# Outputs of an S5 scan: one 128-row product for two of 64 rows

## The chip, the cores and the metric

The kernel runs on one core of a Trainium2 chip. The metric is the device time of one execution in microseconds (us), the median of three runs. Engines: PE (TensorE, matrix products), DVE (VectorE), ACT (ScalarE), POOL (GpSimd), SP (SyncE, which here issues the transfers).

## What is computed

Two layers of a decoder, each with three head groups: HGRN2, gated linear attention and S5. 1,024 prompt tokens go through both layers, and 8 further sequences take one token each from a given state. The change concerns the third group, S5: 16 channel groups of 16 channels, each with 64 complex states x.

```
bu_re = einsum('gpc,btgc->btgp', bb_re, u);  bu_im likewise
x_t   = a * x_(t-1) + bu_t                    (complex, associative scan over t)
y     = einsum('gcp,btgp->btgc', C_re, x_re) - einsum('gcp,btgp->btgc', C_im, x_im) + D * u
```

The outputs y are a sum over 64 real and 64 imaginary parts per channel group.

## The kernel before

Tokens stand in the free dimension, 1,032 in blocks of 384, 384 and 264. Every projection is a loop (`gemm_tile`, L302) over tiles of 128 output channels: for each block, eight slices of the input, each with three products of fp32r halves (`hh`, `lo` by `wh`, `wl`) into a PSUM bank `ps_g`. The halves of the weights are made on the way by `do_split` (L274): ACT copies `wh`, and POOL and DVE in turn subtract to give `wl` (L289). DVE moves a finished bank out (L741).

The recurrences are Python generators ("threads"), and `tick()` lets each emit its next piece between the products of a tile. Slots of the on-chip memory are handed out by `alloc`, `release` and `need`. The order in the engines' queues is then set by the scheduler of the tile framework from the program's order and its own timeline.

`s5_thread` (L467) runs the third group, in two runs (`hf`) per layer of eight channel groups each. Two channel groups share the 128 partitions: `gp` 0 in rows 0 to 63, `gp` 1 in rows 64 to 127, four such pairs q. Tokens are cut into 128 pieces of 8, and a piece's state x is scanned over the pieces. One run goes like this:

- `E_` (powers of the state's rotation, POOL, L488 to L494), `PB` and `Bm` (input matrices), `Tm` (the kernel within a piece).
- `Vt` = `Bm` times the inputs `U` on PE (L558), evicted by ACT (L560).
- The rotation by `E_` on DVE and POOL gives `W_` (L574 to L580, tile name `s5W`); DVE scans it (L584), eight scans.
- The rotation back (`cmul`, six DVE operations, L591) writes the states `Xp` over `Vt` (tile name `s5V`), real parts in `Xp[:, 0]`, imaginary ones in `Xp[:, 1]`; the 8 further sequences' states are copied to columns 128 to 136 (L589).
- The output matrices `O_` (`s5O`, L604 to L609) are made by POOL and DVE.
- The outputs (L613 to L628): for each half q2 of the pairs, a bank `py[gp]` for each channel group sums products of 64 rows, two for each of two pairs (`ri` 0 and 1), and then the products by `Tm` (128 rows, L625). They are plain fp32, and each shows as two records of PE in the trace.

```
for ri in range(2):
    for gp in range(2):
        rr = slice(64 * gp, 64 * gp + 64)
        mm(o(gp, qq), O_[rr, ri, 2 * q2 + qq, :], Xp[rr, ri, 2 * q2 + qq, :], start=(qq + ri == 0), stop=False)
```

In this kernel, layer 0's first run has its outputs at 118 to 128 us and its second at 201 to 207 us; layer 1's are at 624 to 634 and 704 to 711 us.

Of the kernel before, what the change touches and what calls it, by code (L numbers as in the profile page):

```python
# [12 lines left out]
ALU = mybir.AluOpType  # L13

P = 128
# [23 lines left out]
def tile_hybrid_step(ctx: ExitStack, tc: tile.TileContext, a: dict, nl=NL, limit=RANGE):  # L39
# [37 lines left out]
    def release(x):  # L77
        t = tag_of.pop(id(x))
        del owner[t]
        free.append(t)  # L80
# [279 lines left out]
    def cmul(e, dr, di, ar, ai, br, bi, t):  # L360

        e.tensor_tensor(out=dr, in0=ar, in1=br, op=ALU.mult)
        e.tensor_tensor(out=t, in0=ai, in1=bi, op=ALU.mult)
        e.tensor_tensor(out=dr, in0=dr, in1=t, op=ALU.subtract)  # L364
        e.tensor_tensor(out=di, in0=ar, in1=bi, op=ALU.mult)
        e.tensor_tensor(out=t, in0=ai, in1=br, op=ALU.mult)
        e.tensor_tensor(out=di, in0=di, in1=t, op=ALU.add)
# [99 lines left out]
    def s5_thread(l, dd, usd, udd, ud, st, s5w, x0, pw, pv, bb, cbd, so, m8):  # L467
# [4 lines left out]
        for hf in range(2):  # L472
            q0 = 4 * hf
            qs_ = slice(q0, q0 + 4)
# [107 lines left out]
            for ri in range(2):  # L582
                for q in range(4):
                    V.tensor_tensor_scan(out=W_[:, ri, q], data0=m8[:, q0 + q:q0 + q + 1].to_broadcast([P, P]),  # L584
                                         data1=W_[:, ri, q], initial=0.0, op0=ALU.mult, op1=ALU.add)
            Xp = Vt
            t7 = t[:, :, 0:127]
            V.memset(Xp[:, :, :, 0:1], 0.0)
            V.tensor_copy(out=Xp[:, :, :, 128:136], in_=x0[:, :, qs_, :])  # L589
            yield  # L590
            cmul(V, Xp[:, 0, :, 1:128], Xp[:, 1, :, 1:128], W_[:, 0, :, 0:127], W_[:, 1, :, 0:127],  # L591
                 E_[:, 0, :, 0:127], E_[:, 1, :, 0:127], t7)
            cmul(V, sp[:, 0, qs_].unsqueeze(2), sp[:, 1, qs_].unsqueeze(2), W_[:, 0, :, 127:128], W_[:, 1, :, 127:128],
                 E_[:, 0, :, 127:128], E_[:, 1, :, 127:128], t[:, :, 127:128])
            V.tensor_tensor(out=so[:, :, qs_], in0=so[:, :, qs_], in1=sd, op=ALU.add)
            yield from pause(PX)
            release(W_)
            release(E_)
            yield

            yield from need(1)
# [1 line left out]
            c_re, c_im = cs_(s5w[:, 2, qs_]), cs_(s5w[:, 3, qs_])  # L603
            G.tensor_tensor(out=f4(O_[:, 0]), in0=c_re, in1=pws(0, 1), op=ALU.mult)  # L604
            V.tensor_tensor(out=t4, in0=c_im, in1=pws(1, 1), op=ALU.mult)
            G.tensor_tensor(out=O_[:, 0], in0=O_[:, 0], in1=t, op=ALU.subtract)
            G.tensor_tensor(out=f4(O_[:, 1]), in0=c_re, in1=pws(1, 1), op=ALU.mult)
            V.tensor_tensor(out=t4, in0=c_im, in1=pws(0, 1), op=ALU.mult)
            V.scalar_tensor_tensor(out=O_[:, 1], in0=O_[:, 1], scalar=-1.0, in1=t, op0=ALU.mult, op1=ALU.subtract)  # L609
            yield  # L610
            yield from need(0, 1)
            Yt = alloc("s5Y", [P, 8, 136])
            for q2 in range(2):  # L613

                py = [psum("aux") for _ in range(2)]
                o = lambda gp, qq, n=136: py[gp][:, qq * 136:qq * 136 + n]
                for qq in range(2):
                    for ri in range(2):
                        for gp in range(2):
                            rr = slice(64 * gp, 64 * gp + 64)  # L620
                            mm(o(gp, qq), O_[rr, ri, 2 * q2 + qq, :], Xp[rr, ri, 2 * q2 + qq, :], start=(qq + ri == 0), stop=False)
                for gp in range(2):
                    for qq in range(2):
                        g = 2 * (2 * q2 + qq) + gp
                        mm(o(gp, qq, 128), Tm[:, g, :], U[:, g, 0:128], start=False, stop=(qq == 1))  # L625
                for gp in range(2):
                    act(out=Yt.rearrange("p (q g) n -> p g q n", g=2)[:, gp, 2 * q2:2 * q2 + 2, :],
                                 in_=py[gp][:, :272].rearrange("p (q n) -> p q n", q=2), func=AF.Copy)  # L628
                yield
# [1002 lines left out]
```

## Time and profile before

| | |
|---|---|
| median of three runs | 1055.06 us (1053.12 to 1058.06) |
| the profiled execution's own time | 1056.13 us |
| its span, first to last instruction | 1054.2 us |
| PE busy | 994.6 us (94%) |
| DVE, ACT, POOL busy | 649.4, 479.2 and 472.2 us |
| mean granted clock of TensorE | 0.97 |
| chain that ended last | PE 68%, DVE 15%, POOL 7%, ACT 3%, issue 3%, DMA 2% |

All sums are made against the profiled execution. Products are pipelined, and their durations overlap: what one costs in a stream is read from where the next one starts.

### The profile page before, as it was taken

Reading aid. Unit: us, or ns where it says so; the run is one execution under the profiler, and the core shown is the slowest. Engines: PE = TensorE matmul, PEld = TensorE weight load, DVE = VectorE, ACT = ScalarE, POOL = GpSimd, SP = SyncE. Lnnn points to the kernel's source line nnn. Section 1 sums busy time; section 2 is a strip of 40 time slices with the busy share of each in tenths; the row PEclk is TensorE's granted clock in tenths of the full one; section 3 lists DMA queues with packets and bytes.
Section 4 is the critical chain, followed back from the end, with each engine's and each line's share of the span. In section 5 each row is a group of like instructions: output and inputs, shape, how many; then the busy total and the mean of one; then the engine's idle time right before and its main releaser. Section 6 shows DMA issues by size and latency. Waiting matters only on the chain.

```text
span 1054.2 us, 20947 instructions
## 1 busy us (share of the span) xinstructions
PE 994.6 (94%) x8071; PEld 940.2 (89%) x8071; DVE 649.4 (62%) x1333; ACT 479.2 (45%) x995; POOL 472.2 (45%) x668
## 2 busy tenths in 40 slices
PE   6899999999999899999999999999999989999992
PEld 5788898899988799999999999888998988999991
DVE  8986745744767746685464682684388775553344
ACT  7334224554434656633332423445554475664431
POOL 4685754115355535542181476431344453552233
PEclk9999999899999989999999999999999998999996
DMA  7131131111111121144323114112111112112313
GB/s 245 46 107 51 42 107 46 59 50 56 54 40 38 57 73 60 48 137 136 128 78 92 48 41 113 45 47 61 41 56 53 41 53 70 54 48 88 116 51 135
DMA packets 78811, 76.77 MB, mean 73 GB/s; under 512 B 24524, under 2 KB 60652, under 8 KB 78700
## 3 DMA queue, kind: packets, MB, share of 16 engines
q1 hardware_dynamic: 78700, 75.33, 23.6%
q8 instruction: 65, 1.06, 0.4%
q14 instruction: 46, 0.38, 0.1%
HBM read 58.01 MB, written 15.53 MB: 70 GB/s over the span
## 4 chain that ended last, share of the span: by engine, by line
PE 68%; DVE 15%; POOL 7%; ACT 3%; issue 3%; DMA 2%; SPq 1%; DVEq 0%; POOLq 0%; ACTq 0%
PE ps_g L156 54%; PE ps_aux L156 8%; PE ps_o L156 5%; DVE s5W L584 1%; DVE Sp L897 1%; ACT ep L146 1%; DVE ep L873 1%; PE ps_aux L850 1%; POOL wl L289 1%; DVE onorm L1045 1%; DMA x<-in_xT 1%; ACT sg L146 1%; DVE wl L289 1%; DVE sl L907 1%; POOL s5E L364 1%
## 5 line engine op out<-in xcount | busy, mean ns | idle before, releaser
L156 PE MATMUL ps_g<-hh,wl 128*128 128x384 f32 (+1 forms) x1176 | 382.1, 326 | 4.5 <-POOL wl L289 4.5
L156 PE MATMUL ps_g<-hh,wh 128*128 128x384 f32 (+1 forms) x1176 | 384.6, 327 | 0.0
L156 PE MATMUL ps_g<-lo,wh 128*128 128x384 f32 (+1 forms) x1176 | 380.9, 324 | 0.0
L156 PEld LDWEIGHTS ps_g<-hh,wl 128*128 128x128 f32 x1176 | 223.5, 190 | 8.8 <-POOL wl L289 6.8
L156 PEld LDWEIGHTS ps_g<-hh,wh 128*128 128x128 f32 x1176 | 223.7, 190 | 5.3 <-issue 3.1
L156 PEld LDWEIGHTS ps_g<-lo,wh 128*128 128x128 f32 x1176 | 223.8, 190 | 1.0
L289 POOL TENSOR_TENSOR wl<-raw,wh 128x256 fp32r<-128x256 f32 x127 | 109.6, 865 | 219.9 <-ACT wh L146 207.0
L146 ACT ACTIVATE wh<-raw 128x256 fp32r<-128x256 f32 x258 | 102.2, 411 | 123.9 <-PE ps_g L156 111.5
L156 PE MATMUL ps_g<-m,wh 128*128 128x384 f32 (+1 forms) x567 | 135.7, 321 | 0.0
L289 DVE TENSOR_TENSOR wl<-raw,wh 128x256 fp32r<-128x256 f32 x131 | 82.1, 627 | 42.3 <-ACT wh L146 34.5
L156 PEld LDWEIGHTS ps_g<-m,wh 128*128 128x128 f32 x567 | 98.9, 188 | 0.5
L156 PE MATMUL ps_g<-m,wl 128*128 128x384 f32 (+1 forms) x261 | 82.9, 320 | 0.0
L1350 POOL TENSOR_TENSOR z<-z,sg 128x384 f32<-128x384 f32 (+1 forms) x48 | 47.3, 986 | 44.8 <-ACT sg L146 43.6
L156 PEld LDWEIGHTS ps_g<-m,wl 128*128 128x128 f32 x261 | 49.0, 188 | 0.1
L741 DVE TENSOR_TENSOR z<-ps_g,rn 128x384 f32<-128x384 f32 (+1 forms) x48 | 24.4, 509 | 32.8 <-PE ps_g L156 32.7
L146 ACT ACTIVATE sg<-z 128x384 f32<-128x384 f32 (+1 forms) x48 | 23.4, 487 | 28.9 <-DVE z L1348 28.7
L1360 DVE SCALAR_TENSOR_TENSOR onorm<-z,vec,onorm 128x384 f32<-128x384 f32 (+1 forms) x36 | 23.0, 639 | 21.3 <-POOL z L1350 21.2
L156 PE MATMUL ps_g<-vx,wh 128*128 128x384 f32 (+1 forms) x129 | 34.1, 322 | 0.0
L146 ACT ACTIVATE sg<-sg,ones 128x384 f32<-128x384 f32 (+2 forms) x52 | 32.3, 622 | 0.8
L146 ACT ACTIVATE sg<-sg 128x384 f32<-128x384 f32 (+2 forms) x56 | 31.8, 568 | 1.7 <-DVE sg L778 0.8
L156 PE MATMUL ps_o<-qs,Sp 64*64 64x64 f32 x360 | 23.4, 301 | 8.6 <-DVE Sp L897 8.6
L156 PEld LDWEIGHTS ps_o<-qs,Sp 64*64 64x64 f32 x360 | 21.2, 199 | 10.8 <-DVE Sp L897 9.6
(385 smaller groups left out, 1802.1 us busy)
## 6 DMA issues: line engine op xcount, KB each, us to landing
raw<-in_wf SPq DMA_DIRECT2D x100, 256.0 KB
raw<-in_wo SPq DMA_DIRECT2D x32, 256.0 KB
x<-in_xT SPq DMA_DIRECT2D x16, 192.0 KB
ext<-in_xT SPq DMA_DIRECT2D x16, 192.0 KB
x1d<-ext SPq DMA_DIRECT2D x16, 192.0 KB
ext<-x1d SPq DMA_DIRECT2D x16, 192.0 KB
usd<-ucp SPq DMA_DIRECT2D x4, 512.0 KB
s5U<-usd SPq DMA_DIRECT2D x32, 64.0 KB
```

Source lines behind the costliest of these rows:

```text
L146: return S.activation(out=out, in_=in_, func=func, **kw)
L156: return TE.matmul(out=out, lhsT=lhsT, rhs=rhs, start=start, stop=stop)
L289: e.tensor_tensor(out=wl, in0=r, in1=wh.bitcast(F32), op=ALU.subtract)
L364: e.tensor_tensor(out=dr, in0=dr, in1=t, op=ALU.subtract)
L584: V.tensor_tensor_scan(out=W_[:, ri, q], data0=m8[:, q0 + q:q0 + q + 1].to_broadcast([P, P]), data1=W_[:, ri, q], initial=0.0, op0=ALU.mul ...
L741: V.tensor_tensor(out=dst[:, o:o + n], in0=p, in1=rn[:, o:o + n], op=ALU.mult)
L850: TE.transpose(out=p[:, c * P:(c + 1) * P], in_=f[:, t0:t0 + P], identity=ident)
L873: V.tensor_tensor_scan(out=g[:, cs], data0=zero[:pr].to_broadcast([pr, ch]) if plus is None else plus[:, cs], data1=x[:, cs], initial=0.0, ...
L897: V.tensor_tensor_scan(out=s[:, :64 * n], data0=s[:, :64 * n], data1=kv[:, :64 * n], initial=0.0, op0=ALU.mult, op1=ALU.add)
L907: V.tensor_tensor(out=sl, in0=sq, in1=sh.bitcast(F32), op=ALU.subtract)
L1350: G.tensor_tensor(out=z[:, c], in0=z[:, c], in1=sg[:, c], op=ALU.mult)
L1360: V.scalar_tensor_tensor(out=on[:, c], in0=z[:, c], scalar=g, in1=on[:, c], op0=ALU.mult, op1=ALU.mult)
```

## The change

Real and imaginary parts of one channel group are stacked in the 128 rows. `Xp[:, gp]` now holds in rows 0 to 63 the real and in rows 64 to 127 the imaginary parts of channel group `gp`, and `O_[:, gp]` the matrices to match. One product of 128 rows takes the place of two of 64. Four of DVE's operations of the rotation back, two of the matrices' and the copies become operations on 64 partitions that may write to the other half than they read, and there are more of them. `E_` is kept longer, as room for a factor of `O_`.

```diff
-            V.tensor_copy(out=Xp[:, :, :, 128:136], in_=x0[:, :, qs_, :])
+            for ri, to in enumerate((lo_, hi_)):
+                for gp, of in enumerate((lo_, hi_)):
+                    V.tensor_copy(out=Xp[to, gp, :, 128:136], in_=x0[of, ri, qs_, :])
...
-            cmul(V, Xp[:, 0, :, 1:128], Xp[:, 1, :, 1:128], W_[:, 0, :, 0:127], W_[:, 1, :, 0:127],
-                 E_[:, 0, :, 0:127], E_[:, 1, :, 0:127], t7)
+            V.tensor_tensor(out=x7[:, 0], in0=w0, in1=e0, op=ALU.mult)
+            V.tensor_tensor(out=t7, in0=w1, in1=e1, op=ALU.mult)
+            V.tensor_tensor(out=x7[lo_, 1], in0=x7[hi_, 0], in1=t7[hi_], op=ALU.subtract)
+            V.tensor_tensor(out=x7[lo_, 0], in0=x7[lo_, 0], in1=t7[lo_], op=ALU.subtract)
+            V.tensor_tensor(out=e1, in0=w0, in1=e1, op=ALU.mult)
+            V.tensor_tensor(out=t7, in0=w1, in1=e0, op=ALU.mult)
+            V.tensor_tensor(out=x7[hi_, 0], in0=e1[lo_], in1=t7[lo_], op=ALU.add)
+            V.tensor_tensor(out=x7[hi_, 1], in0=e1[hi_], in1=t7[hi_], op=ALU.add)
...
-            G.tensor_tensor(out=O_[:, 0], in0=O_[:, 0], in1=t, op=ALU.subtract)
-            G.tensor_tensor(out=f4(O_[:, 1]), in0=c_re, in1=pws(1, 1), op=ALU.mult)
+            V.tensor_tensor(out=O_[lo_, 1], in0=O_[hi_, 0], in1=t[hi_], op=ALU.subtract)
+            G.tensor_tensor(out=O_[lo_, 0], in0=O_[lo_, 0], in1=t[lo_], op=ALU.subtract)
+            G.tensor_tensor(out=f4(E_[:, 0]), in0=c_re, in1=pws(1, 1), op=ALU.mult)
             V.tensor_tensor(out=t4, in0=c_im, in1=pws(0, 1), op=ALU.mult)
-            V.scalar_tensor_tensor(out=O_[:, 1], in0=O_[:, 1], scalar=-1.0, in1=t, op0=ALU.mult, op1=ALU.subtract)
+            for gp, of in enumerate((lo_, hi_)):
+                V.scalar_tensor_tensor(out=O_[hi_, gp], in0=E_[of, 0], scalar=-1.0, in1=t[of], op0=ALU.mult,
+                                       op1=ALU.subtract)
+            release(E_)
...
-                for qq in range(2):
-                    for ri in range(2):
-                        for gp in range(2):
-                            rr = slice(64 * gp, 64 * gp + 64)
-                            mm(o(gp, qq), O_[rr, ri, 2 * q2 + qq, :], Xp[rr, ri, 2 * q2 + qq, :], start=(qq + ri == 0), stop=False)
+                for gp in range(2):
+                    for qq in range(2):
+                        mm(o(gp, qq), O_[:, gp, 2 * q2 + qq, :], Xp[:, gp, 2 * q2 + qq, :], start=(qq == 0), stop=False)
```

In the changed file the copies are L592, the rotation back L597 to L604, the matrices L615 to L622, and lines behind them stand 12 further down (L741 is L753).

The scheduler then orders the queues anew. On PE, layer 0's first run, from where the output products start in earnest (`ps_g` is the projection going on beside them). Before:

```order
L156 MATMUL ps_aux_1300<-s5V_1055,s5O_1273 128x136
L156 MATMUL ps_aux_1301<-s5V_1055,s5O_1273 128x136
L156 MATMUL ps_aux_1300<-s5V_1055,s5O_1273 128x136
L156 MATMUL ps_aux_1301<-s5V_1055,s5O_1273 128x136
L156 MATMUL ps_aux_1300<-s5V_1055,s5O_1273 128x136
L156 MATMUL ps_aux_1301<-s5V_1055,s5O_1273 128x136
L156 MATMUL ps_aux_1300<-s5U_654,s5T_1160 128x128 x2
L156 MATMUL ps_aux_1301<-s5U_654,s5T_1160 128x128 x2
L156 MATMUL ps_aux_1334<-s5V_1055,s5O_1273 128x136 x4
L156 MATMUL ps_aux_1334<-s5U_654,s5T_1160 128x128 x2
```

Now:

```order
L156 MATMUL ps_aux_1307<-s5V_1055,s5O_1278 128x136 x2
L156 MATMUL ps_aux_1308<-s5V_1055,s5O_1278 128x136 x2
L156 MATMUL ps_aux_1307<-s5U_654,s5T_1160 128x128 x2
L156 MATMUL ps_aux_1308<-s5U_654,s5T_1160 128x128 x2
L867 MATMUL ps_aux_1319<-ident,vf_1062 8x128
L156 MATMUL ps_g_1481<-hh,wh_1368 128x384
```

Before, two products stood 16 places ahead and four more stand 10 places behind this piece, between projection products; products by `s5O` and by `s5T` take turns. Now there are two pieces, this one and a second like it 20 places on, and each piece has all products of a half.

On POOL, layer 0's first run, from the first factor of `O_` to the last rotation of `W_` (`wl` is a weight's split). Before:

```order
L604 TENSOR_TENSOR s5O_1273<-s5w_271,pw_276 128x512
L607 TENSOR_TENSOR s5O_1273<-s5w_271,pw_276 128x512
L575 TENSOR_TENSOR s5W_1162<-s5V_1055,s5E_686 128x512
L579 TENSOR_TENSOR s5W_1162<-s5V_1055,s5E_686 128x512
L289 TENSOR_TENSOR wl_1186<-raw_1101,wh_1185 128x256
L576 TENSOR_TENSOR s5W_1162<-s5W_1162,t_86_653 128x512
L289 TENSOR_TENSOR wl_1266<-raw_1183,wh_1265 128x256
L580 TENSOR_TENSOR s5W_1162<-s5W_1162,t_86_653 128x512
```

Now:

```order
L615 TENSOR_TENSOR s5O_1278<-s5w_271,pw_276 128x512
L575 TENSOR_TENSOR s5W_1162<-s5V_1055,s5E_686 128x512
L579 TENSOR_TENSOR s5W_1162<-s5V_1055,s5E_686 128x512
L576 TENSOR_TENSOR s5W_1162<-s5W_1162,t_86_653 128x512
L289 TENSOR_TENSOR wl_1186<-raw_1101,wh_1185 128x256
L289 TENSOR_TENSOR wl_1271<-raw_1183,wh_1270 128x256
L580 TENSOR_TENSOR s5W_1162<-s5W_1162,t_86_653 128x512
```

The second factor (L607, now L619) has left this place, and a split (`wl_1186`) has moved behind L576.

On POOL, directly behind that, the start of the next run's `E_` and the split that the next projection tile needs (`wl_1370` before, `wl_1369` now). Before:

```order
L488 MEMSET s5E_1448 128x4
L489 MEMSET s5E_1448 128x4
L362 TENSOR_TENSOR s5E_1448<-s5E_1448,pv_277 128x4
L365 TENSOR_TENSOR s5E_1448<-s5E_1448,pv_277 128x4
L363 TENSOR_TENSOR s5Bm_1449<-s5E_1448,pv_277 128x4
L364 TENSOR_TENSOR s5E_1448<-s5E_1448,s5Bm_1449 128x4
L366 TENSOR_TENSOR s5Bm_1449<-s5E_1448,pv_277 128x4
L362 TENSOR_TENSOR s5E_1448<-s5E_1448,pv_277 128x4x2
L365 TENSOR_TENSOR s5E_1448<-s5E_1448,pv_277 128x4x2
L367 TENSOR_TENSOR s5E_1448<-s5E_1448,s5Bm_1449 128x4
L289 TENSOR_TENSOR wl_1370<-raw_1263,wh_1369 128x256
```

Now:

```order
L619 TENSOR_TENSOR s5E_686<-s5w_271,pw_276 128x512
L488 MEMSET s5E_1447 128x4
L489 MEMSET s5E_1447 128x4
L362 TENSOR_TENSOR s5E_1447<-s5E_1447,pv_277 128x4
L365 TENSOR_TENSOR s5E_1447<-s5E_1447,pv_277 128x4
L289 TENSOR_TENSOR wl_1369<-raw_1268,wh_1368 128x256
L618 TENSOR_TENSOR s5O_1278<-s5O_1278,t_86_653 64x512
```

The factor L619, which waits until DVE has read `E_` for the last time, stands first, and the split stands behind four small operations where it stood behind ten. On DVE the split for the same tile's second quarter (L289) moves from ahead of L578 to behind the first four scans.

## Rows read from the trace of the kernel before

**Rows 1.** windows: us, busy us (x instructions) per engine, granted clock, DMA share, GB/s

```profile
95.00:130.00 35.00, 33.69 (x230) 31.71 (x227) 26.82 (x54) 8.42 (x20) 26.65 (x51) 1.00 0.10 34
210.00:250.00 40.00, 40.00 (x291) 37.10 (x290) 17.41 (x31) 23.14 (x35) 10.59 (x10) 1.00 0.18 52
284.00:370.00 86.00, 75.75 (x916) 71.27 (x908) 60.23 (x116) 43.50 (x88) 43.76 (x47) 0.94 0.17 50
```

**Rows 2.** timeline of PE: start us, duration us, engine, line, operation; layer 0, first run

```profile
116.39 0.44 PE L156 MATMUL ps_g<-hh,wl 128*128 128x384 f32 x1 [1.31 <-POOL wl L289]
```

**Rows 3.** timeline of PE, layer 0, first run: the third group's products

```profile
117.72 0.34 PE L156 MATMUL ps_g<-hh,wh 128*128 128x384 f32 x1
117.90 0.34 PE L156 MATMUL ps_g<-lo,wh 128*128 128x384 f32 x1
118.17 0.50 PE L156 MATMUL ps_aux<-s5V,s5O 64*128 64x136 f32 x4
118.60 0.27 PE L855 MATMUL ps_aux<-ident,vf 128*8 128x128 f32 x1
...
121.08 0.97 PE L156 MATMUL ps_aux<-s5V,s5O 64*128 64x136 f32 x12
121.98 1.16 PE L156 MATMUL ps_aux<-s5U,s5T 128*128 128x128 f32 x8
123.07 1.19 PE L156 MATMUL ps_aux<-s5V,s5O 64*128 64x136 f32 x8
124.19 0.71 PE L156 MATMUL ps_aux<-s5U,s5T 128*128 128x128 f32 x4
124.66 0.42 PE L156 MATMUL ps_g<-hh,wh 128*128 128x384 f32 x1
...
126.24 1.19 PE L156 MATMUL ps_aux<-s5V,s5O 64*128 64x136 f32 x8
...
127.83 0.42 PE L156 MATMUL ps_g<-hh,wl 128*128 128x384 f32 x1
```

**Rows 4.** timeline of PE, layer 0, second run: the same products

```profile
201.17 1.20 PE L156 MATMUL ps_aux<-s5V,s5O 64*128 64x136 f32 x16
...
203.38 1.09 PE L156 MATMUL ps_aux<-v,ktmB 128*32 128x64 f32 x32
204.40 1.76 PE L156 MATMUL ps_aux<-s5V,s5O 64*128 64x136 f32 x16
...
207.01 0.42 PE L156 MATMUL ps_g<-hh,wl 128*128 128x384 f32 x1
```

**Rows 5.** timeline of DVE, layer 0, first run

```profile
97.97 1.28 DVE L589 COPY s5V<-x 128x64 f32<-128x64 f32 x1
...
106.46 0.69 DVE L362 TENSOR_TENSOR s5V<-s5W,s5E 128x508 f32<-128x508 f32 x1
107.07 0.68 DVE L365 TENSOR_TENSOR s5V<-s5W,s5E 128x508 f32<-128x508 f32 x1
...
118.39 1.24 DVE L924 COPY qbd<-q 32x8 f32<-32x8 f32 x4
```

**Rows 6.** timeline of POOL, layer 0, first run

```profile
96.38 1.12 POOL L607 TENSOR_TENSOR s5O<-s5w,pw 128x512 f32<-128x512 f32 x1
...
100.49 0.93 POOL L289 TENSOR_TENSOR wl<-raw,wh 128x256 fp32r<-128x256 f32 x1
...
111.87 0.10 POOL L488 MEMSET s5E<- 128x4 f32 x1 [6.35 <-DVE t L366]
...
114.56 1.78 POOL L289 TENSOR_TENSOR wl<-raw,wh 128x256 fp32r<-128x256 f32 x1
```

**Rows 7.** timeline of PE, layer 0, second run: the wait before a transposition

```profile
184.38 0.66 PE L850 MATMUL ps_aux<-ident,vf 128*128 128x128 f32 x4 [1.91 <-DVE atts L1181]
```

**Rows 8.** windows, columns as in rows 1: after that wait, and layer 1's second run

```profile
185.00:192.00 7.00, 7.00 (x41) 5.36 (x41) 7.00 (x24) 3.36 (x8) 0.81 (x2) 0.51 0.01 2
675.00:705.00 30.00, 28.57 (x248) 24.89 (x248) 26.88 (x46) 13.18 (x28) 14.41 (x15) 1.00 0.15 40
```

More of the change, by code (lines that the diff above doesn't have):

```diff
@@ L586, in s5_thread @@
             Xp = Vt
-            t7 = t[:, :, 0:127]
-            V.memset(Xp[:, :, :, 0:1], 0.0)
-            V.tensor_copy(out=Xp[:, :, :, 128:136], in_=x0[:, :, qs_, :])
-            yield
-            cmul(V, Xp[:, 0, :, 1:128], Xp[:, 1, :, 1:128], W_[:, 0, :, 0:127], W_[:, 1, :, 0:127],
-                 E_[:, 0, :, 0:127], E_[:, 1, :, 0:127], t7)
+            lo_, hi_ = slice(0, 64), slice(64, P)
+            V.memset(Xp[:, :, :, 0:1], 0.0)
+            for ri, to in enumerate((lo_, hi_)):
+                for gp, of in enumerate((lo_, hi_)):
+                    V.tensor_copy(out=Xp[to, gp, :, 128:136], in_=x0[of, ri, qs_, :])
+            yield
+            t7 = t[:, :, 0:127]
+            w0, w1, e0, e1 = W_[:, 0, :, 0:127], W_[:, 1, :, 0:127], E_[:, 0, :, 0:127], E_[:, 1, :, 0:127]
+            x7 = Xp[:, :, :, 1:128]
+            V.tensor_tensor(out=x7[:, 0], in0=w0, in1=e0, op=ALU.mult)
[6 more added lines that the diff above has]
+            V.tensor_tensor(out=x7[hi_, 1], in0=e1[hi_], in1=t7[hi_], op=ALU.add)
             cmul(V, sp[:, 0, qs_].unsqueeze(2), sp[:, 1, qs_].unsqueeze(2), W_[:, 0, :, 127:128], W_[:, 1, :, 127:128],
@@ L597, in s5_thread @@
             release(W_)
-            release(E_)
             yield
```

## Prediction

> **What bounds the kernel.** I read the page first, then the windows of PE, then the timelines of PE, DVE and POOL around the four runs of the third group. PE is busy almost everywhere, and beside the third group's outputs it is busy for 33.69 of 35 us, at full clock, with DVE at 26.82 [rows 1]. There the other engines work under a cover: PE goes on with the projection (`ps_g`), and their time counts only where PE runs out of something. In layer 0's first run it does so once: it waits 1.31 us for a weight's split on POOL [rows 2]. So in these stretches a microsecond taken from PE's own queue is a microsecond, and one added to DVE is free until DVE makes PE wait.
>
> **What the products cost now.** In layer 0's second run sixteen records (eight products of 64 rows) take 1.20 us, and sixteen others take 1.76 us [rows 4]. In the first run eight records in a row for one bank take 1.19 us [rows 3]. The trace thus has two kinds: where products for rows 0 to 63 and for rows 64 to 127 alternate, two run at a time; where the scheduler put four for one bank in a row, they run singly. Comparing 16 records in 1.20 us with 4 in 0.50 us [rows 3, 4], twelve more cost 0.70 us, that is 0.117 us for a pair. Products by `s5T` (128 rows) cost 0.1125 us a record: eight take 1.16 us and four 0.71 us [rows 3].
>
> A change of shape costs on top. Two projection products start 0.18 us apart, but the first 64-row product starts 0.27 us after the last of them [rows 3], 0.09 us more. Inside a piece each turn from `s5O` to `s5T` and back is dear too: `s5T`'s eight records stand between 121.98 and 123.07 us [rows 3], 1.09 us, where eight times 0.1125 is 0.90.
>
> **The change on PE.** First run of layer 0: the outputs hold PE from 118.17 to 118.60, 121.08 to 124.66 and 126.24 to 127.83 us [rows 3], together 5.60 us, and three entries add 0.27: 5.87 us. Second run: 201.17 to 203.38 and 204.40 to 207.01 us [rows 4], 4.82 us. Afterwards each run has eight products of 128 rows by `s5O`, 16 records, and the same 16 records by `s5T`. A record of 128 rows and 136 columns isn't in this trace. It is bounded below by the pair's 0.117 us, which reads as many rows and columns, and above by 0.1125 x 136 / 128 = 0.120 us. I take 0.117, the nearer in kind. 16 x 0.117 + 16 x 0.1125 = 3.67 us. All have one shape now, the projection's own, so that entries and turns go. In the second run products of a third shape (`ktmB`) stand in between, so I leave three changes of shape there: 3.67 + 3 x 0.09 = 3.94. Saved: 2.2 and 0.9 us, 3.1 a layer. Layer 1's runs show the same pieces. **6.2 us in all**; with all entries kept (0.09 for each of four pieces a layer, and 0.120 a record) it would be 5.3, with `ktmB`'s gone too and the slower step out of a piece counted 7.2.
>
> A rule bears on this. Half of the old products show that two products of 64 rows run at once [rows 4]. The Trainium skill (TensorEngine Tiling (Array Packing), Key Properties) says that tiles of the array work independently and load and multiply in parallel. By that rule alone a pair always costs what one product of 128 rows does, and stacking wins only the changes of shape: without the eight singles' steps a first run holds (0.94 us) and the 0.56 us of the second, the saving is 6.2 - 3.0 = 3.2 us and the time 1050.6. The trace agrees only where the queue alternates; as the old steps are measured, the sum goes by them, and this end gets no chance of its own.
>
> **The change on DVE.** A run gets four copies of 64 rows for one of 128; the old one took 1.28 us, beside a busy POOL, and four copies to separate row groups elsewhere take 1.24 [rows 5]: from nothing to 1.2 us more. The rotation back has eight long operations for six. They start 0.61 us apart [rows 5], and no row here shows one of half the partitions: if those take as long, 1.2 us more, if they took half, nothing. I take 1.2. The matrices get two more of 512 columns, 1.2 us by the same row. Sum 2.4 us, at most 3.6, for each of four runs: 9.8 to 14.6 us. I cost it at nothing on the path, because PE covers it. DVE has 8.2 us idle in the 35 us of the first run [rows 1] and 3.1 of 30 in layer 1's second run [rows 8]; what the cover's loss would cost is the third rival. Who waits: the eviction of `ps_g` banks, the masks of the second recurrence, and POOL behind the last read of `E_`. L620, which writes the scratch tile again, waits for POOL's L618 as L608 waited for L606; behind it now stand a split and L1125, L1132, and that split is for a later projection tile. The split moved behind four scans is needed only when PE comes to the next tile's second quarter.
>
> **The change on POOL.** As many operations as before, but the order matters. Before L576, on which DVE waits with L578, L607 stood (1.12 us), and a split (0.93 us) [rows 6]; both are gone from there. So DVE's chain can begin up to 2 us earlier. Until its last read of `E_` it then has one long operation more (0.6 us) and the copies (up to 1.2). Behind that read, before: ten small operations from 111.87 us, and the split PE waits for starts at 114.56, 2.69 us on, and takes 1.78 [rows 6]. Now: L619 (as L607, 1.12 us) and four of the ten, by their share 1.1 us: 2.2 us, half a microsecond sooner. Together the split comes between 2.5 us earlier and, if DVE gains nothing at its start, 1.3 us later. As L607 and the split certainly left, I take the early side: **the 1.31 us goes**. The later split would make the wait 2.6 us.
>
> SP's queue gets one or two weight loads moved by a place, ahead of small ones; nothing waits on it in these stretches, so nothing.
>
> **The sum.** -6.2 - 1.3 = -7.5 us. The profiled execution took 1056.13 us, so 1048.6; the median of the runs, 1055.06, lies 1.07 lower, so **1047.6 us**.
>
> **Rivals.**
> 1. *More than that.* In layer 0's second run PE waits 1.91 us for DVE's masks [rows 7], and then runs 7 us at a granted clock of 0.51 [rows 8], the 1.2 GHz level: about 3.4 us lost. DVE's scans stand ahead of those masks, with L604 and L607 on POOL beside them; with L607 later, the scans may end up to 1.1 us sooner. In layer 1's second run the clock is 1.00 throughout [rows 8]. If the wait shrinks and the clock stays: -7.5 - 1.1 - 3.4 = -12, 1043; with the larger saving on PE and a microsecond in layer 1 also, 1041. Against it: whether the clock falls is not in the change's hands.
> 2. *The gain is lost further on.* Between 284 and 370 us PE idles 10.3 us [rows 1], waiting for chains of DVE and ACT in the first group's recurrence. If these start no earlier, PE's lead becomes more idle time: up to all 7.5 us, 1055; half of it, 1051. Against it: from 210 to 250 us PE is busy 40.00 of 40 us [rows 1], so PE sets when that stage begins, and a lead should be handed on. For it: the scheduler has reordered queues in that stage as well.
> 3. *Slower.* DVE becomes the bound of the third group's stretches. The place is the second run, where PE already waits for DVE's masks [rows 7] and DVE has 3.1 us idle in 30 [rows 8] against 2.4 to 3.6 added. It decides once the added work passes that idle time: then evictions and masks move with DVE. With all 14.6 us on the path and 6.2 saved it is +8.4, 1063.5. Against it: most of the added operations stand behind the masks, and PE has projection work to go on with.
> 4. That the products are not really halved can be left out: the new queue holds them, two to a bank.
>
> **How the numbers follow.** The forecast, 1044 to 1050: 0.47. Rival 1, 1040.5 to 1044: 0.12. Rival 2, 1050 to 1056: 0.31. Rival 3, from 1056 up: 0.10. A measurement of this kernel tells about 0.5% from no change, 5.3 us, so faster means below 1049.8: the forecast but for a small part (0.45) and rival 1, 0.57. Same: 0.33. Slower: 0.10. The range goes from rival 1's low end to rival 2's high one, 1040.5 to 1056.5, and leaves rival 3 out. The forecast's own range is 1044 to 1050.
>
> **What would show it.** Right: 64 records of `s5V`, `s5O` in place of 128, with 128 rows, starting about 0.117 us apart, and no step over 0.13 us between them and those of `s5T`; the output pieces of a first run at 3.7 us together; no wait of PE for POOL at the second projection tile's split; DVE busy 10 to 15 us more. Wrong: records of 0.2 us, a new wait of PE for DVE in the second runs, a longer idle time between 284 and 370 us, or one more stretch at half clock.

## Result and profile after

The changed kernel takes **1064.2 us** (median of four runs, 1060.79 to 1074.6); the kernel before, beside it on the same chip, 1054.09. The ratio is **1.0124**, 95% interval [1.0092, 1.0156]: 10 us slower by the medians, 13 by the ratio, where 7.5 us less were forecast. A run is left out of all figures here when it is over 1.5% slower than the fastest of its kernel, which happened once (factor_new_order, 1077.75 us).

The page of the changed kernel, its profiled execution (1060.79 us), begins with busy time, share of the span and instructions of each engine, then come the shares of the chain that ended last:

```profile
span 1058.9 us, 20863 instructions
...
PE 989.5 (93%) x8007; PEld 936.8 (88%) x8007; DVE 673.7 (64%) x1361; ACT 476.9 (45%) x995; POOL 467.6 (44%) x668
...
PE 55%; DVE 22%; POOL 8%; ACT 5%; issue 5%; DMA 3%; SPq 2%; DVEq 0%; POOLq 0%; ACTq 0%
```

PE is busy 5.1 us less than before and DVE 24.3 more, and the span is longer. The share of PE in the chain falls from 68 to 55%, that of DVE rises from 15 to 22%.

The windows that answer to [rows 1] and [rows 8] (us, busy us of PE, PEld, DVE, ACT, POOL, granted clock, DMA share, GB/s):

```profile
95.00:130.00 35.00, 32.95 (x221) 31.61 (x220) 31.68 (x64) 9.51 (x21) 20.08 (x42) 1.00 0.16 48
210.00:250.00 40.00, 38.72 (x287) 36.26 (x284) 17.93 (x31) 23.96 (x36) 8.36 (x8) 1.00 0.19 54
284.00:370.00 86.00, 76.25 (x930) 71.99 (x918) 60.39 (x116) 43.37 (x88) 43.94 (x48) 0.94 0.17 50
185.00:192.00 7.00, 6.22 (x55) 5.13 (x54) 6.97 (x23) 2.57 (x6) 0.83 (x2) 1.00 0.04 3
675.00:705.00 30.00, 28.54 (x268) 24.56 (x267) 26.64 (x48) 12.92 (x28) 14.71 (x17) 1.00 0.15 41
```

In the first run DVE's busy time grows from 26.82 to 31.68 of 35 us. Between 210 and 250 us, where PE had no idle time, it now has 1.28 us; between 284 and 370 little has changed (9.75 us idle for 10.25). From 185 to 192 us the clock is 1.00 where it was 0.51; that part of the first rival came about in this run, and the time grew all the same.

The loss lies in the third group's stretches. The first and the second run of layer 0, then those of layer 1; before:

```profile
95.00:140.00 45.00, 43.69 (x305) 41.07 (x302) 29.62 (x60) 11.70 (x26) 36.33 (x63) 1.00 0.20 61
140.00:215.00 75.00, 73.09 (x687) 63.83 (x686) 43.61 (x85) 29.25 (x59) 24.27 (x31) 0.95 0.25 67
600.00:655.00 55.00, 54.03 (x374) 50.54 (x373) 33.62 (x67) 15.08 (x34) 39.02 (x66) 1.00 0.21 59
655.00:740.00 85.00, 83.57 (x789) 73.00 (x788) 52.09 (x85) 38.40 (x71) 24.18 (x28) 1.00 0.21 58
```

After:

```profile
95.00:140.00 45.00, 42.95 (x295) 40.81 (x294) 32.88 (x67) 10.39 (x23) 30.00 (x58) 1.00 0.21 61
140.00:215.00 75.00, 69.96 (x655) 61.13 (x653) 50.52 (x92) 27.89 (x59) 27.22 (x34) 0.98 0.23 64
600.00:655.00 55.00, 51.81 (x355) 49.15 (x356) 38.69 (x75) 14.12 (x33) 37.63 (x65) 1.00 0.21 56
655.00:740.00 85.00, 78.54 (x734) 68.26 (x733) 53.39 (x87) 34.79 (x66) 24.91 (x30) 0.98 0.21 59
```

PE's idle time (the length less its busy time) grows there from 5.6 to 16.7 us, and most of that in the second runs, from 3.3 to 11.5.

The waits of PE in the whole span (engine, line, what for: us in total, times, longest):

```profile
PE ps_o L156 <- DVE Sp L909: 8.4, 6, 2.3
PE ps_aux L156 <- DVE sl L919: 7.4, 7, 2.5
...
PE ps_g L156 <- POOL wl L289: 3.7, 6, 1.3
PE ps_aux L156 <- DVE kst L531: 3.1, 2, 1.6
PE ps_aux L156 <- ACT s5Y L146: 2.9, 2, 1.9
PE ps_g L156 <- DVE wl L289: 2.7, 2, 1.4
```

Before, `sl` (the head norm) cost 4.2 us in 4 waits; those for `kst`, `s5Y` and DVE's `wl` are not in the list at all. On PE, the product of [rows 2], which now starts at 112.95 us, the one six products on with a wait for DVE, the new output piece, and the wait for `kst`:

```profile
112.95 0.45 PE L156 MATMUL ps_g<-hh,wl 128*128 128x384 f32 x1 [0.67 <-POOL wl L289]
...
115.62 0.44 PE L156 MATMUL ps_g<-hh,wl 128*128 128x384 f32 x1 [1.36 <-DVE wl L289]
...
119.12 1.42 PE L156 MATMUL ps_aux<-s5V,s5O 128*128 128x136 f32 x8
120.38 1.05 PE L156 MATMUL ps_aux<-s5U,s5T 128*128 128x128 f32 x8
121.27 0.27 PE L867 MATMUL ps_aux<-ident,vf 128*8 128x128 f32 x1
...
143.31 0.48 PE L156 MATMUL ps_aux<-kst,t 16*128 16x128 f32 x2 [1.61 <-DVE kst L531]
...
145.12 0.52 PE L156 MATMUL ps_g<-lo,wh 128*128 128x384 f32 x1
```

PE still waits 0.67 us for POOL's split, half of the old wait, and the 1.36 us for DVE's are new. Behind the wait for `kst` the next projection products take 0.52 us for 0.34: half clock, for 3.4 us. Why DVE's split comes late is seen on DVE. First run:

```profile
95.18 3.89 DVE L592 COPY s5V<-x 64x32 f32<-64x32 f32 x4
...
107.28 0.68 DVE L600 TENSOR_TENSOR s5V<-s5V,t 64x508 f32<-64x508 f32 x1
107.89 0.67 DVE L601 TENSOR_TENSOR s5E<-s5W,s5E 128x508 f32<-128x508 f32 x1
...
109.80 0.68 DVE L603 TENSOR_TENSOR s5V<-s5E,t 64x508 f32<-64x508 f32 x1
110.50 1.50 DVE L604 TENSOR_TENSOR s5V<-s5E,t 64x508 f32<-64x508 f32 x1
...
112.62 0.82 DVE L616 TENSOR_TENSOR t<-s5w,pw 128x512 f32<-128x512 f32 x1
113.48 0.69 DVE L617 TENSOR_TENSOR s5O<-s5O,t 64x512 f32<-64x512 f32 x1
114.19 1.38 DVE L289 TENSOR_TENSOR wl<-raw,wh 128x256 fp32r<-128x256 f32 x1
...
118.29 1.41 DVE L622 SCALAR_TENSOR_TENSOR s5O<-s5E,t 64x512 f32<-64x512 f32 x2
```

POOL, beside the four copies, and further on:

```profile
94.66 1.75 POOL L579 TENSOR_TENSOR s5W<-s5V,s5E 128x512 f32<-128x512 f32 x1
96.37 1.27 POOL L576 TENSOR_TENSOR s5W<-s5W,t 128x512 f32<-128x512 f32 x1
97.61 1.42 POOL L289 TENSOR_TENSOR wl<-raw,wh 128x256 fp32r<-128x256 f32 x2
...
115.25 0.91 POOL L289 TENSOR_TENSOR wl<-raw,wh 128x256 fp32r<-128x256 f32 x1
119.84 0.20 POOL L363 TENSOR_TENSOR s5Bm<-s5E,pv 128x4 f32<-128x4 f32 x1 [3.68 <-DVE s5O L622]
```

The slot that `E_` leaves is the next run's `Bm`, and POOL uses `Bm` as room for the powers. Since `E_` now comes free behind L622, POOL waits 3.68 us. The next run's powers end at 142.1 us, for 134.1 before (the last L367), and `kst` is summed 0.8 us behind them. But this is not the hold's doing: with `E_` free early in the same order of the queues they end hardly sooner, at 142.2 us in both_new_order and 142.9 in factor_new_order (both among the experiments). The last L367 of both_new_order, then of the changed kernel:

```profile
141.42 0.74 POOL L367 TENSOR_TENSOR s5E<-s5E,s5Bm 128x256 f32<-128x256 f32 x1
```

```profile
141.41 0.73 POOL L367 TENSOR_TENSOR s5E<-s5E,s5Bm 128x256 f32<-128x256 f32 x1
```

With the old work in the new order (order_only) they end at 139.2 us: the order brings 5.1 of the 8 us, and DVE's additions the rest.

### The profile page after: what moved, and what is told of

Its sections match the earlier page's. It is cut to its first block, busy times and chain, and to the rows that moved or that the text cites. A ratio compares the mean times of both kernels' runs of the same rounds, so it can differ in the third digit from the quotient of the medians.

```text
span 1058.9 us, 20863 instructions
## 1 busy us (share of the span) xinstructions
PE 989.5 (93%) x8007; PEld 936.8 (88%) x8007; DVE 673.7 (64%) x1361; ACT 476.9 (45%) x995; POOL 467.6 (44%) x668
## 4 chain that ended last, share of the span: by engine, by line
PE 55%; DVE 22%; POOL 8%; ACT 5%; issue 5%; DMA 3%; SPq 2%; DVEq 0%; POOLq 0%; ACTq 0%
PE ps_g L156 46%; PE ps_aux L156 4%; PE ps_o L156 4%; DVE Sp L909 2%; DVE ep L885 1%; DVE s5W L584 1%; DMA x<-in_xT 1%; ACT ep L146 1%; DVE wl L289 1%; DVE s5V L592 1%; POOL s5E L364 1%; SPq L549 1%; DVE onorm L1057 1%; POOL s5Bm L366 1%; POOL s5Bm L363 1%
## 5 line engine op out<-in xcount | busy, mean ns | idle before, releaser
L156 PEld LDWEIGHTS ps_g<-hh,wl 128*128 128x128 f32 x1176 | 223.3, 190 | 11.2 <-POOL wl L289 6.0
L289 POOL TENSOR_TENSOR wl<-raw,wh 128x256 fp32r<-128x256 f32 x127 | 105.4, 831 | 207.6 <-ACT wh L146 196.7
L289 DVE TENSOR_TENSOR wl<-raw,wh 128x256 fp32r<-128x256 f32 x131 | 78.9, 603 | 33.5 <-ACT wh L146 24.5
L1372 DVE SCALAR_TENSOR_TENSOR onorm<-z,vec,onorm 128x384 f32<-128x384 f32 (+1 forms) x36 | 24.9, 690 | 28.8 <-POOL z L1362 28.8
L753 DVE TENSOR_TENSOR z<-ps_g,rn 128x384 f32<-128x384 f32 (+1 forms) x48 | 24.4, 508 | 20.5 <-PE ps_g L156 20.3
L1451 DVE TENSOR_TENSOR lo<-ps_g,ext 128x384 f32<-128x384 f32 (+1 forms) x24 | 12.3, 512 | 30.3 <-PE ps_g L156 30.2
```

What stands on the lines that cost most here:

```text
L156: return TE.matmul(out=out, lhsT=lhsT, rhs=rhs, start=start, stop=stop)
L289: e.tensor_tensor(out=wl, in0=r, in1=wh.bitcast(F32), op=ALU.subtract)
L753: V.tensor_tensor(out=dst[:, o:o + n], in0=p, in1=rn[:, o:o + n], op=ALU.mult)
L1372: V.scalar_tensor_tensor(out=on[:, c], in0=z[:, c], scalar=g, in1=on[:, c], op0=ALU.mult, op1=ALU.mult)
L1451: V.tensor_tensor(out=x, in0=p, in1=xo, op=ALU.add)
```

## Experiments

Two theories stood at the start. **A**: the longer hold of `E_` delays the second run. **B**: DVE's added work is on the path. The first results brought **C**, that the scheduler's new order of all queues costs the time, against **D**, the change's own work.

Runs of one kernel differ by up to 14 us, and most of that goes with TensorE's clock: the changed kernel's run of 1060.79 us had a mean granted clock of 0.974, that of 1074.6 had 0.965. So the table has, beside the time, the time **net of the clock**, as a mean over a kernel's runs: the device time less span x (1 - mean granted clock). There a microsecond at half clock counts half; what is taken off is called lost to the clock. (The expectations call it span times the mean granted clock; that product itself is about 1.9 us lower for every kernel.) Its standard error is 0.2 for the kernel before (81 runs) and 0.4 to 1.2 us for the others (4 to 12 runs). It is a way of counting, not a measurement: it takes it that whatever ran at half clock would have taken half as long. And a clock that falls because of a change is part of what the change costs, so the time itself has to be read beside it.

| kernel | order of the queues | median, us | ratio to before, 95% | clock | net of the clock, us |
|---|---|---|---|---|---|
| before | own | 1052.8 | | 0.973 | 1024.3 |
| after | own | 1064.2 | 1.0124 [1.0092, 1.0156] | 0.971 | 1035.1 |
| factor_elsewhere | own | 1065.2 | 1.0122 [1.0086, 1.0158] | 0.970 | 1033.7 |
| hold_only | own | 1050.3 | 0.9980 [0.9962, 0.9998] | 0.977 | 1026.9 |
| products_only | own | 1062.4 | 1.0094 [1.0062, 1.0125] | 0.965 | 1024.9 |
| operands_only | own | 1062.7 | 1.0100 [1.0072, 1.0128] | 0.971 | 1031.2 |
| same_order | before's | 1068.0 | 1.0147 [1.0117, 1.0177] | 0.964 | 1028.7 |
| products_same_order | before's | 1054.6 | 1.0017 [0.9998, 1.0036] | 0.971 | 1023.6 |
| relieved | before's | 1052.4 | 0.9994 [0.9975, 1.0013] | 0.973 | 1024.1 |
| order_only | after's | 1049.2 | 0.9981 [0.9957, 1.0006] | 0.973 | 1020.7 |
| products_new_order | after's | 1058.0 | 1.0049 [1.0029, 1.0068] | 0.966 | 1022.5 |
| matrices_new_order | after's | 1060.1 | 1.0073 [1.0044, 1.0102] | 0.969 | 1027.1 |
| rotation_new_order | after's | 1057.0 | 1.0040 [1.0020, 1.0060] | 0.973 | 1028.9 |
| both_new_order | after's | 1062.6 | 1.0092 [1.0072, 1.0112] | 0.973 | 1032.8 |
| one_copy | after's | 1066.7 | 1.0146 [1.0125, 1.0167] | 0.967 | 1032.1 |
| factor_new_order | after's | 1070.7 | 1.0174 [1.0133, 1.0214] | 0.966 | 1033.8 |
| relieved_new_order | after's | 1047.8 | 0.9966 [0.9943, 0.9988] | 0.974 | 1020.3 |

### First: the parts apart, each in the scheduler's own order

**factor_elsewhere**

```diff
             O_ = alloc("s5O", [P, 2, 4, P])
+            yield from need(0, 1)
+            Yt = alloc("s5Y", [P, 8, 136])
+            F_ = Yt[:, 0:4, 0:P]
...
-            G.tensor_tensor(out=f4(E_[:, 0]), in0=c_re, in1=pws(1, 1), op=ALU.mult)
+            G.tensor_tensor(out=f4(F_), in0=c_re, in1=pws(1, 1), op=ALU.mult)
```

> The changed kernel, but the second factor of the matrices (GpSimd's product) is written into the block of the outputs Yt, allocated a little earlier, instead of into E_, and E_ is released where it was before the change. Theory A (the buffer held longer): the second run's rotation powers on GpSimd start near 112 us again instead of 120.5, both waits of PE for the DVE sum of kst (3.1 us over the two layers) are gone, and the time is 1047 to 1054 us, at least 7 us under the changed kernel. Theory B (the added DVE work): the buffer costs nothing that lasts, the time stays at 1060 to 1065.

1065.2 us, and PE still waits for `kst` (2.5 us in two waits). Theory A's number is not there.

**hold_only**

```diff
-            G.tensor_tensor(out=f4(O_[:, 1]), in0=c_re, in1=pws(1, 1), op=ALU.mult)
+            G.tensor_tensor(out=f4(E_[:, 0]), in0=c_re, in1=pws(1, 1), op=ALU.mult)
...
-            V.scalar_tensor_tensor(out=O_[:, 1], in0=O_[:, 1], scalar=-1.0, in1=t, op0=ALU.mult, op1=ALU.subtract)
+            V.scalar_tensor_tensor(out=O_[:, 1], in0=E_[:, 0], scalar=-1.0, in1=t, op0=ALU.mult, op1=ALU.subtract)
+            release(E_)
```

> The kernel before with nothing but the hold: GpSimd's product goes into E_ and the last DVE instruction of the matrices reads it there, so that E_ comes free behind it; 128 products of 64 rows and all operands as before. Theory A: the waits of PE for the DVE sum of kst appear (2 of about 1.5 us), rotation powers near 120 us, and the time is 1058 to 1066 us. Theory B: 1053 to 1056, as before.

1050.3 us, faster than before if anything. The hold alone costs no time (net of the clock 2.6 us more, in an order of its own); **theory A falls**.

**products_only** has the product loop of the change and all else of the kernel before, **operands_only** the reverse:

```diff
+                for gp in range(2):
+                    for qq in range(2):
+                        mm(o(gp, qq), O_[:, gp, 2 * q2 + qq, :], Xp[:, gp, 2 * q2 + qq, :], start=(qq == 0), stop=False)
```

> The kernel before with the 64 products of 128 rows alone, on operands laid out as before (so the sums mix other rows than the reference's; nothing is added on DVE and E_ is released early). Both theories: the term of the prediction without its costs, 1046 to 1050 us. If it is 1053 or more, the saving on PE is lost further on in any case (the prediction's second rival).

> The changed kernel's operands, with its DVE work and its hold of E_, but the 128 products of 64 rows of before (on rows laid out otherwise, so the sums aren't the reference's). The price of the operands alone: the changed kernel's time plus what the products save, 1066 to 1073 us by both theories; under 1062, the products save less here than forecast.

Both 9 to 10 us slower than before, and the first was to be the forecast without its costs. Half as many products on PE, and nothing else touched, made the kernel slower. Since each of these kernels is scheduled anew, the order of the queues differs from run to run of this table, and theory C came up.

### Second: the order held fixed

The queues were pinned: behind the whole program each instruction is tied to the one ahead of it in the wanted order of its queue, without a wait.

```diff
+    here = {i.name: i for i in nc.cur_bb.bb.instructions}
...
+        for x, y in zip(names, names[1:]):
+            tc.add_manual_dep(here[y], x, mybir.DependencyInfo(mybir.DependencyClass.NoSync, mybir.DependencyReason.DATA),
+                              reason="order")
```

> The change with its factor in Yt's block, and every queue pinned to the order of the kernel before: each instruction that both have stands where it stood, the new ones stand at the places of those they replace (the vd transposition, which shares PE's small banks, follows the products in the first runs). Theory C (the scheduler's new order of the queues costs the time, not the change's work): 1045 to 1051 us, the forecast after all, with PE's waits as in the kernel before. Theory D (the change's own work costs it, whatever the order): 1058 us or more.

> The 64 products of 128 rows alone, on operands laid out as before (the sums mix other rows than the reference's), with every queue pinned to the order of the kernel before. The same kernel in the scheduler's own order took 1062.4 us. Theory C: 1045 to 1050 us, so about 15 us are the order's. Theory D: 1058 us or more. Between them the saving on PE is read off: 6 us below the kernel before by the prediction's term.

> The kernel before with its own 128 products, copies, rotation back and matrices, but every queue pinned to the order that the scheduler gave the changed kernel; E_ comes free early. Theory C: slower than the kernel before without any of the change's work, 1058 to 1066 us. Theory D: 1051 to 1057 us.

The change in the old order is the slowest so far (1068.0), and the old work in the new order the fastest (1049.2). **Theory C falls, D stands**, though only same_order lies in one of the ranges set ahead (D's): the order that the scheduler chose is even 3.6 us better net of the clock, and by time not worse (the interval reaches 1.0006). In the old order products_same_order and same_order differ by the new operands alone (and the places of their instructions), and these cost 13.4 us (1054.6 to 1068.0; net of the clock 5.1). That C had something in it is seen from products_only, which took 1062.4 us in its own order and 1054.6 in that of before; 6 of these 8 us were lost to the clock. And in both fixed orders the halved products save nothing: net of the clock they change -0.7 us in the old order and +1.8 in the new one, and by time they cost 2 us (about the error) and 9.

### Third: the change's parts in the changed kernel's order

**one_copy** loads the start states a second time, stacked, and needs one copy again:

```diff
+            if hf == 0:
+                for ri in range(2):
+                    SY.dma_start(out=x0[64 * ri:64 * ri + 64], in_=a["x0"][l][:, ri].rearrange("(g p) q b -> p g q b", g=2))
...
+            V.tensor_copy(out=Xp[:, :, :, 128:136], in_=x0[:, :, qs_, :])
```

**factor_new_order** and **products_new_order** are factor_elsewhere and products_only, pinned; **both_new_order** is one_copy and factor_new_order together.

> The changed kernel in its own order, with one DVE copy of 128 rows per run for the further sequences' states again, as before: the start states are loaded a second time by SP, already stacked. Theory E (the four copies, which took 14.4 us of DVE against 3.4 before, are the largest part of the loss): 1055 to 1059 us. If it stays at 1062 to 1066, the copies are covered.

> The changed kernel with its factor in Yt's block and E_ free early, and every queue in the changed kernel's order, so that only GpSimd's wait for the last DVE instruction of the matrices goes. Theory A, in what is left of it (the hold costs, and in factor_elsewhere another order hid it): 1056 to 1060 us, no wait of PE for kst near 142 us. Otherwise 1062 to 1066.

> The 64 products of 128 rows on operands made as before (the sums mix other rows than the reference's), every queue in the changed kernel's order. Against order_only (1049.2 us, the same order with 128 products) it prices the products once more: 1042 to 1045 us if the 6 us of the prediction show, 1047 to 1051 if the saving is lost as in products_same_order.

> one_copy and factor_new_order together, in the changed kernel's order. Theory E and theory A adding up: 1049 to 1054 us. If neither counts, 1061 to 1066, and what is left is the four long DVE instructions of a run that the rotation back and the matrices gained.

both_new_order came out as if neither theory counted (1062.6), one_copy and factor_new_order no faster than the changed kernel, and products_new_order slower than either theory had it. The wait for `kst` near 142 us is gone in factor_new_order, and the time isn't better for it. By time the copies and the hold are worth nothing singly; net of the clock 3.0 and 1.3 us, both at once 2.3, with errors of 1.1, 1.5 and 1.1. So the four copies, with the largest share of DVE's added time, are not the main loss. What is left between products_new_order and both_new_order, 10.3 us net of the clock and 4.6 by the medians of time, are four long DVE instructions per run.

products_new_order also shows where PE's saving goes. Windows of order_only (128 products) and then of products_new_order (64), the same place in layer 0, columns as above:

```profile
150.00:154.00 4.00, 2.60 (x36) 1.86 (x34) 4.00 (x5) 0.28 (x1) 2.67 (x3) 1.00 0.17 59
154.00:171.00 17.00, 17.00 (x149) 14.26 (x145) 5.53 (x11) 5.96 (x13) 3.29 (x5) 0.90 0.16 39
```

```profile
150.00:154.00 4.00, 0.99 (x20) 0.58 (x20) 3.55 (x5) 0.28 (x1) 2.35 (x2) 0.91 0.05 15
154.00:171.00 17.00, 17.00 (x83) 13.96 (x84) 3.98 (x8) 2.53 (x6) 1.74 (x4) 0.52 0.07 15
```

PE came to the second group's recurrence earlier, and waited there: 1.75 us for DVE's `onorm` and 1.35 for `Sp`, where order_only waits 1.30 once. Its timeline:

```profile
151.66 0.43 PE L156 MATMUL ps_aux<-dS,qbd 128*32 128x64 f32 x16 [1.75 <-DVE onorm L1155]
...
153.99 1.56 PE L156 MATMUL ps_o<-qb,Sp 32*64 32x128 f32 x12 [1.35 <-DVE Sp L895]
```

From 153.3 us, within the second wait, the clock stood at half for 17.1 us, for 3.4 us in order_only, at a PE that was busy all the time from 154 us on: 83 records in those 17 us for 149. This profiled execution (1065.08 us, clock 0.959) is the slowest of the kernel's nine, so not every run has such stretches.

### Fourth: which of DVE's additions, and is it DVE

**matrices_new_order** is both_new_order with the old `cmul` for the rotation back, **rotation_new_order** with the old code of the matrices. **relieved** moves two small copies of the kernel before to ACT, **relieved_new_order** does the same in the changed kernel's order:

```diff
-            V.tensor_copy(out=sd, in_=Vt[:, :, :, 128:136])
+            act(out=sd, in_=Vt[:, :, :, 128:136], func=AF.Copy)
...
-            V.tensor_copy(out=Xp[:, :, :, 128:136], in_=x0[:, :, qs_, :])
+            act(out=Xp[:, :, :, 128:136], in_=x0[:, :, qs_, :], func=AF.Copy)
```

> both_new_order with the rotation back of the kernel before (six long DVE instructions; the states are then not stacked, and the sums aren't the reference's), so that of DVE's additions only those of the matrices are left. Beside the time, the span times the mean granted clock is compared, which leaves out what the clock alone costs: 1032.8 us in both_new_order, 1022.5 in products_new_order, which has none of the additions. Theory M (the matrices' two more long instructions, ahead of the products in DVE's queue, make PE wait): 1029 to 1033 here, and 1059 to 1063 us of time. Theory R (the rotation's two more do): 1022 to 1026, and 1053 to 1058.

> both_new_order with the matrices of the kernel before (not stacked, the sums aren't the reference's), so that only the rotation's additions are left. Theory R: span times clock 1029 to 1033 us, time 1059 to 1063. Theory M: 1022 to 1026, time 1053 to 1058. If each gives about half, 1027 to 1029 in both kernels, it is DVE time as such.

> The kernel before in its own order, with its two small copies per run (L571 and L589, 4.95 and 3.35 us of DVE in all) on ACT, behind the last eviction of Vt. If DVE bounds the third group's stretches, the opposite of the change must show: 1045 to 1050 us. If PE does, no change: 1051 to 1055.

> order_only (1049.2 us) with the same two copies on ACT. If DVE bounds: 1042 to 1047 us, and a version that beats both kernels. If PE does: 1048 to 1051.

Net of the clock, against products_new_order (1022.5), the matrices' additions cost 4.6 us and the rotation's 6.4, together 11.0, and both at once 10.3: **they add up**, and each lies in the range set for DVE time as such. From products_new_order to both_new_order the instructions' durations on DVE grow by 5.3 us for the matrices (from 11.2 to 16.5) and by 5.4 for the rotation (from 17.2 to 22.6), so net of the clock about all of it came back. The time itself says less: 1060.1 and 1057.0 us lie in the ranges that theory M gave for it, and the rotation's additions, 6.4 net of the clock, come out as 1 us less, since products_new_order lost 35.7 us to the clock and rotation_new_order 28.9. Pairs that lost the same are free of this choice: order_only, rotation_new_order and both_new_order lost 28.8, 28.9 and 29.2 us, and their mean times are 1049.5, 1057.9 and 1062.0. So products and rotation together cost 8.4 us and the matrices 4.1 more; how the 8.4 divide is not shown. A kernel with the new operands and the old products in this order, which would tell, was not run; operands_only, in an order of its own, took 9.9 us more than before.

The two relieved kernels changed nothing by more than the error (-0.2 and -0.4 us net of the clock), though they take two copies, 8.3 us in the kernel before, off DVE. By the ranges set ahead this speaks for PE as the bound, and not for DVE (the 1047.8 us of relieved_new_order lie between its two ranges). So it isn't any DVE time: in the first run L578, behind both copies, waits 1.19 us for POOL's L576 in the kernel before and in relieved alike, and a copy beside which DVE would wait for POOL anyway is free, or nearly so, to add (one_copy) as to take away. relieved_new_order is the one kernel that beats both, 0.9966 [0.9943, 0.9988]; most of that is order_only's order.

## Why the prediction was wrong

**The sum**, in the changed kernel's order, as differences of the means (before, order_only, products_new_order, both_new_order, after):

| step | time, us | net of the clock | lost to the clock |
|---|---|---|---|
| the new order | -2.8 | -3.6 | +0.8 |
| the products | +8.7 | +1.8 | +6.9 |
| matrices and rotation | +3.8 | +10.3 | -6.5 |
| copies and hold | +4.0 | +2.3 | +1.7 |
| together | +13.7 | +10.8 | +2.9 |

The whole is not the clock's: the 2.9 us lost to it are hardly more than their error (2.4; the changed kernel has four runs). But between the products and DVE's additions the two ways of counting divide it differently. What holds in both is that the products save nothing and that the additions cost time.

**The products on PE: right in size, and worth nothing.** The trace has 64 records of 128 rows, and within a piece most follow each other at 0.116 us; 0.117 was taken. Several pieces, the one at 119.12 us among them, have steps of 0.19 to 0.30 us inside, and the last piece of layer 1 ran at half clock (0.23), so the sign "no step over 0.13" failed there. PE's busy time fell by 5.1 us. What failed is the first paragraph's sentence that a microsecond taken from PE's own queue is a microsecond. In [rows 1] PE is busy 33.69 of 35 us, but it isn't the engine that sets the pace: behind the stretch it waits for DVE (`onorm`, `Sp`, `sl`), and comes to these waits sooner. Rival 2 had this and gave it the wrong place: the idle time between 284 and 370 us is as before, and PE's lead was gone by 228 us: the same projection product starts at 228.01 us before and at 227.96 after.

**POOL's wait of 1.31 us: half gone, and another put beside it.** PE still waits 0.67 us for POOL's split. And six products on it needs the split of the tile's next quarter, which DVE makes; the prediction speaks of DVE's split for the second quarter, and not of this one. It had fallen behind L604, L616 and L617 in DVE's queue, took 1.38 us itself, and PE waits 1.36 us for it, in both layers. Together 2.0 us in layer 0's first run, for 1.31.

**DVE's additions, costed at nothing: the step that failed most.** The sizes first: 9.8 to 14.6 us in all were forecast; DVE's busy time grew by 24.3. The half-row instructions last as long as full ones (0.68 us for 64 as for 128 partitions), which the prediction took. Not foreseen were that the rotation's L603 and L604 last longer beside POOL's work (1.02 and 1.09 us in the mean), and the copies, 14.4 us for 3.4: each of the four takes up to 1.27 us beside POOL's products and 0.17 at the least. The copy's row [rows 5] could have told it: 1.28 us for 64 elements is no copying time, and four such copies are four such waits. Then the cover. The prediction asked how much idle time DVE has in the windows [rows 1, 8]; but the added instructions stand one behind the other between the scans and the products, with the splits that PE needs behind them. That DVE had 8.2 us idle in 35 helped little, since most of that idle time lies elsewhere. DVE before, with one of its splits for comparison:

```profile
102.89 1.21 DVE L578 TENSOR_TENSOR t<-s5V,s5E 128x512 f32<-128x512 f32 x1 [1.19 <-POOL s5W L576]
...
113.45 0.42 DVE L289 TENSOR_TENSOR wl<-raw,wh 128x256 fp32r<-128x256 f32 x1
...
117.78 0.69 DVE L608 TENSOR_TENSOR t<-s5w,pw 128x512 f32<-128x512 f32 x1 [2.02 <-POOL s5O L606]
...
128.80 0.56 DVE L741 TENSOR_TENSOR kb<-ps_g,rn 128x384 f32<-128x384 f32 x1 [3.42 <-PE ps_g L156]
```

1.19 us stand ahead of the scans and 3.42 behind the matrices; only the 2.02 ahead of L608 lie in the chain that got longer. In both fixed orders the operands then cost time: 13.4 us from products_same_order to same_order (net of the clock 5.1), 4.6 from products_new_order to both_new_order (10.3), where nothing had been forecast.

**Rival 3 was it**, with a chance of 0.10: DVE becomes the bound of the third group's stretches, 1063.5 us. Its price counted 14.6 us of DVE on the path and 6.2 saved on PE; measured were 4.6 by time (10.3 net of the clock) for matrices and rotation, nothing saved, and sums that it hadn't, for the copies and for the clock. So its number, within 1 us of the median, was good partly by chance. Its place, the second runs, was right: 8.2 of PE's 11.1 us of added idle time lie there.

**The hold of `E_`** was named among those who wait (POOL behind the last read of `E_`), but followed only to the split. POOL does wait 3.68 us for it, but the second run's powers end at 142.1 us with it and at 142.2 without it (both_new_order), so PE's 3.1 us for `kst` come from the new order and DVE's additions. That the hold costs nothing that shows in the time was found by hold_only and factor_new_order.

**The clock.** "One more stretch at half clock" stood among the signs of an error, and the kernels with fewer products alone have it: 31.1, 35.7 and 37.5 us lost in products_same_order, products_new_order and products_only, for 28.0 before. It doesn't follow the number of products by itself: rotation_new_order and both_new_order, which have 64 as well, lost 28.9 and 29.2. Why the clock falls in the one and not in the other stays open.

## What to carry to other kernels

An engine that is busy 95% of a stretch need not bound it: ask which engine it waits for at the stretch's end, and price the change on that one first. Idle time in a window covers an addition only if it lies in the chain where the addition stands. And when a scheduler orders the queues, no two versions differ in one thing only; pin the order before a part is priced, and where the clock moves, read the time net of it beside the time itself: a price on which the two disagree is not yet known.

## What the runs showed of the hardware

- **A wait of PE can cost more than itself.** In the profiled run of products_new_order the granted clock fell to the 1.2 GHz level after 3 us of waits within 4, and stayed there for 17.1 us, with PE busy 17.00 of 17.00 us. Two such stretches, one in each layer, cost that run some 17 us, a microsecond at half clock counted half. That a kernel with less PE work is so slowed was not expected.
- **A DVE instruction on the other half of the partitions starts late.** Behind L599, which reads rows 64 to 127, L600 (rows 0 to 63) starts 0.70 us later, behind its end; L601 behind L600, both from row 0, starts 0.61 us later, before L600 has ended. L604 stands 0.70 behind L603. The Trainium skill (VectorE: DVE Perf Modes, Two Vector instructions with no wait between them) says that an instruction whose input or output starts in another quadrant than those of the last one is held until all earlier ones have finished; the trace agrees, at 0.09 us a case.
- **Small copies wait for POOL.** The 64x32 copies took between 0.17 and 1.27 us. The Trainium skill (SBUF — State Buffer, Who interferes with whom) says that DVE's copies in a two-port mode and GpSimd share a port pair, and the one that comes second is blocked for the whole of the other's instruction. The trace agrees with the blocking: the four copies at 95.18 us took 3.89 us together while POOL ran from one product into the next, and each ended 0.04 us behind the end of one of POOL's instructions (L579, L576 and the two splits); in which mode the copies ran, no row shows. That these 11 us were nearly free in the end, one_copy showed.
